# An MLP by seven products per block pair: token halves of 512 and 520 instead of 516 and 516

## The chip, the cores and the metric

One core of a Trainium2 chip. The metric is device time in microseconds (us) of one execution of the whole kernel, as the median of several runs. A profile of one execution stands beside it.

## The reference

A decoder trunk of two layers over 1024 prompt tokens and 8 sample tokens (1032 in all), width 1024, everything in float32. Layer 0 mixes tokens by a gated linear recurrence, layer 1 by sliding-window attention. Each layer ends in an MLP, which is all that the change touches:

```python
def sq_relu_mlp(x, w_up, w_down):
    return jnp.square(jax.nn.relu(x @ w_up)) @ w_down

    ...
        yp = yp + sq_relu_mlp(rms_norm(yp, norm_mlp_g[layer]), mlp_w_up[layer], mlp_w_down[layer])
        ys = ys + sq_relu_mlp(rms_norm(ys, norm_mlp_g[layer]), mlp_w_up[layer], mlp_w_down[layer])
```

`w_up` is 1024 x 4096 and `w_down` 4096 x 1024. The prompt's and the samples' tokens are stacked to 1032 columns, features lie on the 128 partitions.

## The kernel before

**Seven products.** Each MLP is written with Winograd's form of Strassen's scheme: a pair of 128-row blocks of weights and the two halves of the tokens form a 2 x 2 block product, which needs seven products instead of eight. The weights' blocks A11 to A22 are combined into S1 to S4 on VectorE (L498), the tokens' blocks B11 to B22 into T1 to T4. `BY` (L452) says which product uses which operands: 1 is A11 B11, 2 is A12 B21, 3 is S4 B22, 4 is A22 T4, 5 is S1 T1, 6 is S2 T2, 7 is S3 T3. H0 and H1 are the two token halves, both 516 columns wide (`HALF`).

**Three passes.** TensorE takes its operands rounded; to keep float32 accuracy every operand is split into a rounded part and a rest: ScalarE rounds it (a cast, L396 for weights and L402 for stored sums), VectorE subtracts (L397, L403). A product is then three passes, high x high, high x low and low x high, over j blocks of the contraction. Each pass of each j is two matmuls of 258 columns (`QT`), because a bank of PSUM holds 512 float32 columns and 516 don't fit: `product`, L525 to L533.

**Stages.** The up-projection has 16 block pairs q (`NPAIR`), with j over 4 blocks, so 7 x 4 x 3 x 2 = 168 matmuls a pair. The hidden vectors of the first 14 pairs (`NSP`) are combined again, by `sums_of` (L570), and stored to HBM (`hsum`) by DMAs that ScalarE issues; the last two pairs go to `hid` as they are. The down-projection runs over 5 chunks of the contraction (three pairs each, two in the last), with 4 output pairs in each, 126 or 84 matmuls a pair; the output tiles of the first four chunks are added into HBM by accumulating DMAs that GpSimd issues (L656), those of the last chunk take what has been added there (L658). What remains of the contraction, the two pairs in `hid`, follows as a plain matrix product in `down_steps` (L315).

**Order.** `PROG` is the list of products as TensorE runs them, and the loop at L611 goes through it: it makes the operands that are due (`pw.take`), issues the matmuls, evacuates, and asks for the weights' splits of the next products (`pw.look`, by the list `SOON`). The first two pairs are interleaved (their token operands are made at the same time, `tok.make`); after that each pair runs in the order 1, 2, 6, 7, 5, 4, 3. The instructions of an engine are put in an order by the framework's scheduler; `high_priority` and `issue_after` steer it.

**Banks.** PSUM has 8 banks, and a product uses two at a time (`DB`): tag G twice, X once, Y once. Partial sums are shared: U2 = P1 + P6 and so on are accumulated in the bank of an earlier product after ScalarE has copied the earlier value out (L637), and VectorE adds the other ones (L639, L641, L643, L645). The results go to two tiles of a pair, `he` and `ho`, of 1032 columns each. In up, a relu with the norm's factor (L649, VectorE) and a square (L650, ScalarE) follow.

**Loads in the down-projection.** While a chunk runs, `Ahead.fetch` loads the stored sums of the next one (`tl`, L543, DMAs that GpSimd issues), and `Ahead.split` splits them four or five products later. SyncE issues the loads of the weights (L160). Token tiles come from a pool `ap` of 33 buffers, weights' splits from `wp` with 12, and most `he` tiles of the down-projection from the two spare buffers of `rp`.

Of the kernel before, what the change touches and what calls it, by code (L numbers as in the profile page):

```python
# [27 lines left out]
HALF = T // 2  # L28
# [3 lines left out]
QT = T // 4  # L32
# [28 lines left out]
def trunk(ctx: ExitStack, tc: tile.TileContext, I, O):  # L61
# [31 lines left out]

    def A(s="a"):
        return ap.tile([P, T], F32, tag="A", name=nm(s))
# [18 lines left out]
    def DB(tag):  # L114
        return psum["pool"].tile([P, 1024], F32, tag="D" + tag, bufs=2 if tag == "G" else 1, name=nm("bD"))
# [18 lines left out]
    aux = cp.tile([P, CH], F32, name="aux")  # L134
# [255 lines left out]

    H0, H1 = slice(0, HALF), slice(HALF, T)


    def op_of(src, alloc, n):
        t = alloc("op")
        act.copy(r_(t[:, 0:n]), src)  # L396
        dve.tensor_tensor(r_(t[:, n:2 * n]), src, t[:, 0:n], ALU.subtract)  # L397
        return t[:, 0:n], t[:, n:2 * n]
# [8 lines left out]
    class TokenOps:  # L407
        def __init__(self, xs):
            self.pairs = [(xs[2 * j], xs[2 * j + 1]) for j in range(4)]
            self.ops = {n: [] for n in ("B11", "B21", "T3", "T2", "T1", "T4", "B22")}  # L410

# [5 lines left out]
        def early(self, m):  # L417
            j = m // 2
            if m < 4:
                self.make("B11", [m])  # L420
            if m >= 6:
                self.make("B21", (2 * m - 12, 2 * m - 11))
            e, o = self.pairs[j]
            if m % 2 == 0:
                dve.tensor_tensor(e[:, H0], e[:, H1], e[:, H0], ALU.subtract)
            else:
                dve.tensor_tensor(e[:, H1], o[:, H1], e[:, H1], ALU.subtract)

        def B11(self, e, o, j):
            return op_of(e[:, H0], A, HALF)  # L430

        def B21(self, e, o, j):
            return op_of(o[:, H0], A, HALF)

        def B22(self, e, o, j):
            return op_of(o[:, H1], A, HALF)

        def T3(self, e, o, j):
            return op_of(e[:, H1], A, HALF)

        def T2(self, e, o, j):
            dve.tensor_tensor(e[:, H1], o[:, H1], e[:, H0], ALU.subtract)
            return op_of(e[:, H1], A, HALF)

        def T1(self, e, o, j):
            return op_of(e[:, H0], A if j else W, HALF)

        def T4(self, e, o, j):
            dve.tensor_tensor(o[:, H0], o[:, H0], e[:, H1], ALU.subtract)
            return op_of(o[:, H0], A, HALF)  # L450
# [18 lines left out]
    class PairWeights:  # L469
        def __init__(self, layer):  # L470
            self.layer = layer
            self.builds = []
            for key in dict.fromkeys((kind, q) for kind, q, _ in PROG):
                names = ["A11", "A12", "+S1", "+S2", "+S3", "S2", "+S4", "A22", "S3", "S1", "S4"]
                if key in (("up", 0), ("up", 1)):
                    names = ["A11", "A12", "+S1", "+S2", "+S3", "+S4", "A22", "S4", "S3", "S2", "S1"]
                self.builds += [(key, n) for n in names]
            self.src = {}
            self.ops = {}
            self.n = 0  # L480
# [20 lines left out]
        def build(self, upto):  # L501
            while self.n < min(upto, len(self.builds)):
                key, name = self.builds[self.n]
                if name[0] == "+":
                    self.source(key, name[1:])
                else:
                    x = self.source(key, name)
                    self.ops[key, name] = op_of(x, W, self.src[key]["w"])
                self.n += 1
# [15 lines left out]
    def product(d, first, w, xs):  # L525
        n = len(xs)
        for j, (xh, xl) in enumerate(xs):
            for a, (wt, xt) in enumerate(((w[0], xh), (w[0], xl), (w[1], xh))):
                for b in range(2):
                    pe.matmul(d[:, 512 * b:512 * b + QT], lhsT=r_(wt[:, j * P:j * P + P]),  # L530
                              rhs=r_(xt[:, QT * b:QT * b + QT]),
                              start=first and j == 0 and a == 0, stop=j == n - 1 and a == 2,
                              skip_group_check=not first)  # L533
# [7 lines left out]
    def load(src, n):  # L541
        t = A("tl")
        pool.dma_start(t[:, n:2 * n], src)  # L543
        return t[:, 0:n], t[:, n:2 * n]

    PLACE = {n: slice(k * HALF, (k + 1) * HALF) for k, n in enumerate(("B11", "T3", "B21", "B22", "T1", "T2", "T4"))}
# [3 lines left out]
    class Ahead:  # L550
# [6 lines left out]
        def fetch(self, c, upto, step):  # L557
            done = 7 * len(CHUNKS[c]) - len(self.left[c])
            for _ in range(max(0, min(upto - done, len(self.left[c])))):
                name, p = self.left[c].pop(0)  # L560
                self.raw.append((step, c, name, load(self.sums[p][:, PLACE[name]], HALF)))
# [8 lines left out]
    def sums_of(e, o, to):  # L570
        t = small["pool"].tile([P, T], F32, tag="U", name=nm("ts"))

        def put(k, x):
            act.dma_start(to[:, k * HALF:k * HALF + x.shape[1]], x)

        put(2, o)
# [3 lines left out]
        dve.tensor_tensor(t[:, H1], o[:, H1], t[:, H0], ALU.subtract)  # L580
        yield
        put(0, e)
        put(4, t)
        dve.tensor_tensor(o[:, H0], o[:, H0], t[:, H1], ALU.subtract)
        yield
        put(6, o[:, H0])
# [3 lines left out]
    def mlp_products(layer, tok, pw, r, spill, acc, gnext, after):  # L590
# [20 lines left out]
        for n, (kind, q, i) in enumerate(PROG):  # L611
            up = kind == "up"
            w, x = BY[i]
            if up and n in (1, 3, 5, 7, 9):
                tok.make(("B22", "T3", "T2", "T1", "T4")[n // 2])
            if n == 6:
                factors(rs.pop("late"), DB("Y"))
                swap_small(f"u{layer}", 3)
            if (kind, q, i) == ("up", NSP, 5):
# [3 lines left out]
            if i == 1:  # L623
                st[q] = {2: DB("X" if first and q == 1 else "Y"), "g": DB("G"),
                         "e": spare("he") if not up and q in range(2, 12) else A("he"), "o": A("ho")}
            z = st[q]
            alone = i in (1, 2, 7) or (i == 3 and first)
            if alone and i in (3, 7):
                z[i] = DB("Y" if first and q == 0 else "X")
            d = z["g"] if i in (1, 5, 6) else z[7] if i == 4 else z.get(i, z["g"])  # L630
            product(d, alone, wt, (tok if up else ahead).ops[x] if up else ahead.ops[q // 4][x])
            e, o, g = z["e"], z["o"], inner(z["g"])
            e0, e1, o0, o1 = [quarters(t[:, h]) for t in (e, o) for h in (H0, H1)]
            if i in (1, 6, 7, 3):
                t, f = {1: (e0, g), 6: (o0, g), 7: (o1, inner(d)), 3: (e1, inner(d))}[i]
                with tc.high_priority():
                    last["copy"] = act.copy(t, f).ins  # L637
            if i == 2:
                dve.tensor_tensor(e0, inner(d), e0, ALU.add)  # L639
            elif i == 5:  # L640
                dve.tensor_tensor(o1, g, o1, ALU.add)  # L641
                if 3 in z:
                    dve.tensor_tensor(e1, g, e1, ALU.add)  # L643
            elif i == 4:
                dve.tensor_tensor(o0, inner(d), o0, ALU.add)  # L645
            ready = {4: "o", 3: "" if alone else "e", 5: "e" if 3 in z else ""}.get(i, "")
            if ready and up:
                t = z[ready]
                dve.scalar_tensor_tensor(t, t, 0.0, r, ALU.min, ALU.mult)  # L649
                act.activation(t, t, AF.Square)  # L650
                if q >= NSP:
                    act.dma_start(hid[layer][2 * (q - NSP) + (ready == "o")], t)
            elif ready:
                m, t = 2 * (q % 4) + (ready == "o"), z[ready]
# [5 lines left out]
            if i == (4 if 3 in z else 3):  # L660
# [6 lines left out]
            if up and q == NPAIR - 1:  # L667
                k = ORDER.index(i)
                ahead.fetch(0, 3 * (k + 1), n)
                ahead.split(n)  # L670
            elif not up:
                c, k = q // 4, 7 * (q % 4) + ORDER.index(i)
# [591 lines left out]
    hsum = [tc.dram_tile([NSP, P, 7 * HALF], F32, name=f"hsum{i}") for i in range(2)]  # L1264
# [161 lines left out]
```

## Time and profile before

| | us |
|---|---|
| median of 3 runs | 2003.95 (2003.02 to 2004.08) |
| the profiled execution | 2002.95 |
| its span, from the first to the last instruction | 2001.2 |
| TensorE busy | 1987.5 (99%) |
| VectorE busy | 1394.0 (70%) |
| ScalarE busy | 1021.0 (51%) |
| GpSimd busy | 364.4 (18%) |
| TensorE's matmuls of the MLP products (L530), both layers | 648.2 and 568.0 |

The granted clock of TensorE is 1.000 on average. In the profile PE is TensorE's matmuls, PEld its loads of weights, DVE VectorE, ACT ScalarE, POOL GpSimd, SP SyncE; ACTq, SPq and POOLq are DMAs that these engines issue. A group's row reads: line, engine, operation, what is written <- what is read, shape, count | busy us, mean ns of one | idle time of the engine just before them, and what ended it. Matmuls overlap, so that the busy time of a group is less than its count times its mean. The first MLP runs from about 335 to 942 us, the second from about 1344 to 1952 us.

### The profile page before, as it was taken

Reading aid. Unit: us, or ns where it says so; the run is one execution under the profiler, and the core shown is the slowest. Engines: PE = TensorE matmul, PEld = TensorE weight load, DVE = VectorE, ACT = ScalarE, POOL = GpSimd, SP = SyncE. Lnnn points to the kernel's source line nnn. Section 1 sums busy time; section 2 is a strip of 40 time slices with the busy share of each in tenths; the row PEclk is TensorE's granted clock in tenths of the full one; section 3 lists DMA queues with packets and bytes.
Section 4 is the critical chain, followed back from the end, with each engine's and each line's share of the span. In section 5 each row is a group of like instructions: output and inputs, shape, how many; then the busy total and the mean of one; then the engine's idle time right before and its main releaser. Section 6 shows DMA issues by size and latency. Waiting matters only on the chain.

```text
span 2001.2 us, 38937 instructions
## 1 busy us (share of the span) xinstructions
PE 1987.5 (99%) x15188; PEld 1954.1 (98%) x15188; DVE 1394.0 (70%) x2649; ACT 1021.0 (51%) x2021; POOL 364.4 (18%) x664
## 2 busy tenths in 40 slices
PE   9999999999999999999999999999999999999999
PEld 8999999999999999999999897999999999999999
DVE  8996638877675877666846768478767667666662
ACT  7576535543433655545545656455434336554550
POOL 2320000000001233221006658000000003323220
PEclk9999999999999999999999999999999999999999
DMA  5111242343435778877444535623443447888773
GB/s 180 53 43 53 77 147 78 128 164 125 161 127 204 233 211 217 236 198 173 129 106 108 136 98 170 206 81 108 149 154 133 159 149 250 219 221 220 191 194 107
DMA packets 117929, 305.04 MB, mean 152 GB/s; under 512 B 17512, under 2 KB 50032, under 8 KB 117744
## 3 DMA queue, kind: packets, MB, share of 16 engines
q1 hardware_dynamic: 61744, 135.55, 22.0%
q0 software_dynamic: 28352, 98.30, 19.1%
q10 hardware_dynamic: 27648, 68.70, 9.4%
q8 instruction: 119, 1.95, 0.4%
q14 instruction: 66, 0.54, 0.1%
HBM read 176.30 MB, written 113.51 MB: 145 GB/s over the span
## 4 chain that ended last, share of the span: by engine, by line
PE 96%; DVE 1%; POOL 1%; ACT 1%; issue 1%; DMA 0%; SPq 0%; DVEq 0%; POOLq 0%; ACTq 0%
PE bD L530 61%; PE bP L227 13%; PE bS L227 8%; PE bP L793 5%; PE bT L227 4%; PE bS L867 1%; PE bO L916 1%; PE bS L823 1%; PE bT L893 1%; PE bP L893 1%; DMA raw<-w_in 0%; POOL se L883 0%; PE bN L757 0%; DVE sq L278 0%; POOL bias L870 0%
## 5 line engine op out<-in xcount | busy, mean ns | idle before, releaser
L530 PE MATMUL bD<-op,op 128*128 128x258 f32 x5376 | 648.2, 283 | 0.0
L530 PEld LDWEIGHTS bD<-op,op 128*128 128x128 f32 x5376 | 647.7, 190 | 0.3
L530 PE MATMUL bD<-tl,op 128*128 128x258 f32 x4704 | 568.0, 283 | 0.0
L530 PEld LDWEIGHTS bD<-tl,op 128*128 128x128 f32 x4704 | 566.8, 190 | 1.0 <-ACT he L637 0.3
L543 POOL DMA_DIRECT2D tl<-hsum x196 | 115.3, 695 | 899.7 <-PE bD L530 423.0
L397 DVE TENSOR_TENSOR op<-ws,op 128x512 fp32r<-128x512 f32 (+2 forms) x288 | 170.4, 597 | 81.2 <-ACT op L396 81.2
L403 DVE TENSOR_TENSOR tl<-tl 128x516 fp32r<-128x516 f32 x196 | 130.8, 693 | 122.1 <-ACT tl L402 119.5
L637 ACT COPY ho<-bD 128x516 f32<-128x516 f32 x144 | 85.0, 590 | 245.2 <-PE bD L530 240.1
L396 ACT CAST op<-ws 128x512 fp32r<-128x512 f32 (+2 forms) x288 | 155.8, 550 | 56.0 <-DVE op L397 27.1
L397 DVE TENSOR_TENSOR op<-raw,op 128x512 fp32r<-128x512 f32 (+2 forms) x216 | 124.2, 595 | 57.7 <-ACT op L396 57.7
L637 ACT COPY he<-bD 128x516 f32<-128x516 f32 x144 | 83.9, 583 | 133.5 <-PE bD L530 122.2
L396 ACT CAST op<-raw 128x512 fp32r<-128x512 f32 (+2 forms) x216 | 114.5, 549 | 33.4 <-PE bD L530 22.6
L402 ACT CAST tl<-tl 128x516 fp32r<-128x516 f32 x196 | 114.9, 627 | 3.9 <-DMA tl<-hsum 3.8
L650 ACT ACTIVATE ho<-ho 128x1032 f32<-128x1032 f32 x32 | 34.2, 1069 | 107.3 <-DVE ho L649 107.3
L167 DVE TENSOR_TENSOR wl<-raw,wh 128x1024 fp32r<-128x1024 f32 (+1 forms) x57 | 66.0, 1164 | 25.8 <-ACT wh L166 16.6
L876 DVE CUSTOM_DVE_ANT_0 se<-bS,bias,nsink 128x256 f32<-128x256 f32 (+1 forms) x128 | 63.9, 522 | 20.9 <-PE bP L893 7.3
L879 ACT ACTIVATE se<-se,den 128x257 f32<-128x257 f32 (+1 forms) x128 | 62.9, 493 | 29.2 <-DVE den L876 21.7
L166 ACT CAST wh<-raw 128x1024 fp32r<-128x1024 f32 (+1 forms) x60 | 58.6, 987 | 36.9 <-PE bT L227 12.4
L656 POOL DMA_DIRECT2D spill<-ho x32 | 28.4, 889 | 237.7 <-DVE ho L645 229.2
L870 POOL TENSOR_SCALAR bias<-con,aux 128x256 f32<-128x256 f32 (+1 forms) x128 | 64.2, 503 | 41.2 <-DVE den L876 16.8
L793 PE MATMUL bP<-hh,wh 128*128 128x344 f32 x192 | 70.0, 364 | 0.0
L645 DVE TENSOR_TENSOR ho<-bD,ho 128x516 f32<-128x516 f32 x72 | 49.7, 690 | 22.9 <-PE bD L530 22.9
(320 smaller groups left out, 3767.5 us busy)
## 6 DMA issues: line engine op xcount, KB each, us to landing
tl<-hsum POOLq DMA_DIRECT2D x196, 258.0 KB, 8.1
raw<-w_up SPq DMA_DIRECT2D x64, 512.0 KB, 3.7
raw<-w_dn SPq DMA_DIRECT2D x64, 384.0 KB, 6.3
spill<-ho POOLq DMA_DIRECT2D x32, 516.0 KB, 6.6
spill<-he POOLq DMA_DIRECT2D x32, 516.0 KB, 8.6
hsum<-ho ACTq DMA_DIRECT2D x28, 516.0 KB, 3.6
hsum<-he ACTq DMA_DIRECT2D x28, 516.0 KB, 2.7
hsum<-ts ACTq DMA_DIRECT2D x28, 516.0 KB, 3.5
```

Of the source, the lines that this page charges most:

```text
L167: eng.tensor_tensor(r_(lo[:, sl]), raw[:, sl], hi[:, sl], ALU.subtract)
L227: pe.matmul(o, lhsT=r_(wt[:, col(k):col(k) + P]), rhs=r_(xt[:, cs(c)]), start=(k == first and a == 0), stop=(k == final and a == 2))
L396: act.copy(r_(t[:, 0:n]), src)
L397: dve.tensor_tensor(r_(t[:, n:2 * n]), src, t[:, 0:n], ALU.subtract)
L402: act.copy(r_(hi), lo)
L403: dve.tensor_tensor(r_(lo), lo, hi, ALU.subtract)
L530: pe.matmul(d[:, 512 * b:512 * b + QT], lhsT=r_(wt[:, j * P:j * P + P]), rhs=r_(xt[:, QT * b:QT * b + QT]), start=first and j == 0 and a = ...
L543: pool.dma_start(t[:, n:2 * n], src)
L637: last["copy"] = act.copy(t, f).ins
L793: pe.matmul(o, lhsT=r_(wt[:, k * P:k * P + P]), rhs=r_(xt[:, cs(c)]), start=(k == 0 and a == 0), stop=(k == M8 - 1 and a == 2))
L870: pool.tensor_scalar(bias2[:, o - n:o], distM[:, 256 - n:256], fac[:, t % 4, 1, b, u:u + 1], SLOPES[hd[u]], ALU.mult, ALU.mult)
L876: dve.tensor_tensor_reduce(se[:, u, 256 - n:256], s[:, u * 256:u * 256 + n], bias2[:, o - n:o], scale=fac[:, t % 4, 0, b, u:u + 1], scalar ...
```

## The change

The token halves become 512 prompt tokens (H0) and 512 prompt tokens with the 8 samples (H1, 520 columns). Operands of H0 alone (B11, B21, T4) have 512 columns, and their products, 1, 2 and 4, are one matmul of 512 columns for each pass; those with H1 (B22, T1, T2, T3), products 3, 5, 6 and 7, are two of 260. Where blocks of different widths are combined, the samples' columns count as zero in H0: they are copied (8 columns) instead of added, and product 6's evacuation takes product 1's value with 8 columns cleared behind it.

The banks: a single-bank tag Z, twice, for products 1, 2 (added onto 1) and 4; a double-bank tag D, three times, for 6, 7, and 5 with 3 (added onto 5). The steady order becomes 1, 6, 2, 7, 4, 5, 3, with product 1 of the next pair ahead of product 3; the last pair of each projection ends 4, 5, 2, 3. The first two pairs run 1, 2, 3, 7, 6, 4, 5, each product for both. Loads of stored sums follow the new order of use. Tiles of pool `ap` grow from 1032 to 1040 columns; the tile `aux` is given up and lies on the states tile.

The core of the diff:

```diff
-HALF = T // 2
+HW = SEQ // 2
+W1 = T - HW
+TW = 2 * W1
-QT = T // 4
+QT = W1 // 2
...
-    def DB(tag):
-        return psum["pool"].tile([P, 1024], F32, tag="D" + tag, bufs=2 if tag == "G" else 1, name=nm("bD"))
+    def DB():
+        return psum["pool"].tile([P, 1024], F32, tag="D", bufs=3, name=nm("bD"))
+
+    def ZB():
+        return psum["pool"].tile([P, 512], F32, tag="Z", bufs=2, name=nm("bZ"))
...
-    aux = cp.tile([P, CH], F32, name="aux")
...
-    H0, H1 = slice(0, HALF), slice(HALF, T)
+    H0, H1 = slice(0, HW), slice(HW, T)
+    HP, HS = slice(HW, SEQ), slice(SEQ, T)
...
-    ORDER = (1, 2, 6, 7, 5, 4, 3)
+    ORDER = (1, 6, 2, 7, 4, 5, 3)
+    FINAL = (1, 6, 7, 4, 5, 2, 3)
     SOON = (8, 9, 10, 11, 12, 13, 15)
-    PROG = [("up", q, i) for q in (0, 1) for i in (1, 2)] + [("up", q, i) for i in (3, 7, 6, 5, 4) for q in (0, 1)]
-    PROG += [("up", q, i) for q in range(2, NPAIR) for i in ORDER]
+    PROG = [("up", q, i) for i in (1, 2, 3, 7, 6, 4, 5) for q in (0, 1)]
+
+    def steady(kind, qs):
+        out = []
+        for q in qs:
+            for i in ORDER if q != qs[-1] else FINAL:
+                if i == 3 and q != qs[-1]:
+                    out.append((kind, q + 1, 1))
+                if i != 1 or q == qs[0]:
+                    out.append((kind, q, i))
+        return out
+
+    PROG += steady("up", range(2, NPAIR))
     NUP = len(PROG)
-    PROG += [("dn", b, i) for b in range(4 * len(CHUNKS)) for i in ORDER]
+    PROG += steady("dn", range(4 * len(CHUNKS)))
...
-                names = ["A11", "A12", "+S1", "+S2", "+S3", "S2", "+S4", "A22", "S3", "S1", "S4"]
+                names = ["A11", "+S1", "+S2", "S2", "+S3", "+S4", "A12", "S3", "A22", "S1", "S4"]
...
-                for b in range(2):
-                    pe.matmul(d[:, 512 * b:512 * b + QT], lhsT=r_(wt[:, j * P:j * P + P]),
-                              rhs=r_(xt[:, QT * b:QT * b + QT]),
+                c = HW if xt.shape[1] == HW else QT
+                for b in range(xt.shape[1] // c):
+                    pe.matmul(d[:, 512 * b:512 * b + c], lhsT=r_(wt[:, j * P:j * P + P]),
+                              rhs=r_(xt[:, c * b:c * b + c]),
...
-                tok.make(("B22", "T3", "T2", "T1", "T4")[n // 2])
+                tok.make(("B22", "T3", "T2", "T4", "T1")[n // 2])
...
-            d = z["g"] if i in (1, 5, 6) else z[7] if i == 4 else z.get(i, z["g"])
-            product(d, alone, wt, (tok if up else ahead).ops[x] if up else ahead.ops[q // 4][x])
...
-            if i in (1, 6, 7, 3):
-                t, f = {1: (e0, g), 6: (o0, g), 7: (o1, inner(d)), 3: (e1, inner(d))}[i]
-                with tc.high_priority():
-                    last["copy"] = act.copy(t, f).ins
-            if i == 2:
-                dve.tensor_tensor(e0, inner(d), e0, ALU.add)
-            elif i == 5:
-                dve.tensor_tensor(o1, g, o1, ALU.add)
-                if 3 in z:
-                    dve.tensor_tensor(e1, g, e1, ALU.add)
-            elif i == 4:
-                dve.tensor_tensor(o0, inner(d), o0, ALU.add)
...
+            if i == 3 and not first:
+                d = z["d"]
+            elif i in (3, 5, 6, 7):
+                d = z["d"] = DB()
+            else:
+                d = ZB() if i == 4 else z["z"]
+            product(d, i != 2 and (i != 3 or first), wt, tok.ops[x] if up else ahead.ops[q // 4][x])
+            with tc.high_priority():
+                if i == 1:
+                    last["copy"] = act.copy(e0, d).ins
+                elif i == 6 and not first:
+                    with tc.issue_after(last["sum"]):
+                        dve.memset(e[:, HW:W1], 0.0)
+                    dve.tensor_tensor(o1, inner(d), quarters(e[:, 0:W1]), ALU.add)
+                    act.copy(e[:, H1], o[:, H1])
+                elif i == 6:
+                    for t, p in ((o1, o[:, HP]), (e1, e[:, HP])):
+                        dve.tensor_tensor(t, inner(d), t, ALU.add)
+                        dve.tensor_tensor(p, e0, p, ALU.add)
+                    last["copy"] = act.copy(e0, z["z"]).ins
+                elif first and i in (3, 7):
+                    last["copy"] = act.copy(e1 if i == 3 else o1, inner(d)).ins
+                elif i == 4:
+                    dve.tensor_tensor(o0, d, o[:, HP], ALU.add)
+                elif i == 2 and not first:
+                    last["copy"] = act.copy(e0, d).ins
+                else:
+                    for t in ((o1, e1) if first else (e1,) if i == 3 else (o1,)) if i != 2 else ():
+                        last["sum"] = dve.tensor_tensor(t, inner(d), t, ALU.add).ins
...
+    cp8 = cp.tile([P, 4, NS], F32, name="cp8")
     sp.dma_start(st, I["states"])
+    aux = st.rearrange("p m n -> p (m n)")[:, 0:CH]
```

In `sums_of` and in the token operands the samples' columns are handled by copies of 8 columns beside the subtractions, as in

```diff
-        dve.tensor_tensor(t[:, H0], e[:, H1], e[:, H0], ALU.subtract)
+        dve.tensor_tensor(t1, e[:, HP], e[:, H0], ALU.subtract)
+        dve.tensor_copy(t1s, e[:, HS])
```

More of the change, by code (lines that the diff above doesn't have):

```diff
@@ L92, in nm, with A2 @@
         return f"{s}{cnt[0]}"
+    def A2(s="a"):
+        return ap.tile([P, TW], F32, tag="A", name=nm(s))
     def A(s="a"):
-        return ap.tile([P, T], F32, tag="A", name=nm(s))
+        return A2(s)[:, 0:T]
     def W(s="w"):
@@ L388, in out_proj, with op_of @@
         return xs, need, entry_steps(lambda m: ws[m], srcs, xs, gname, r, spill, **kw)
-    H0, H1 = slice(0, HALF), slice(HALF, T)
-    def op_of(src, alloc, n):
+    H0, H1 = slice(0, HW), slice(HW, T)
+    HP, HS = slice(HW, SEQ), slice(SEQ, T)
+    def op_of(src, alloc, *more):
+        n = sum(x.shape[1] for x in (src, *more))
         t = alloc("op")
-        act.copy(r_(t[:, 0:n]), src)
-        dve.tensor_tensor(r_(t[:, n:2 * n]), src, t[:, 0:n], ALU.subtract)
+        at = 0
+        for x in (src, *more):
+            hi, lo = t[:, at:at + x.shape[1]], t[:, n + at:n + at + x.shape[1]]
+            act.copy(r_(hi), x)
+            dve.tensor_tensor(r_(lo), x, hi, ALU.subtract)
+            at += x.shape[1]
         return t[:, 0:n], t[:, n:2 * n]
@@ L410, in __init__ @@
             self.ops = {n: [] for n in ("B11", "B21", "T3", "T2", "T1", "T4", "B22")}
+            self.samples = cp8
         def make(self, name, js=range(4)):
@@ L541, in load @@
     def load(src, n):
-        t = A("tl")
+        t = A2("tl")
         pool.dma_start(t[:, n:2 * n], src)
         return t[:, 0:n], t[:, n:2 * n]
-    PLACE = {n: slice(k * HALF, (k + 1) * HALF) for k, n in enumerate(("B11", "T3", "B21", "B22", "T1", "T2", "T4"))}
+    PLACE = {}
+    for n, w in (("B11", HW), ("T3", W1), ("B21", HW), ("B22", W1), ("T1", W1), ("T2", W1), ("T4", HW)):
+        at = max((x.stop for x in PLACE.values()), default=0)
+        PLACE[n] = slice(at, at + w)
     class Ahead:
@@ L560, in fetch @@
                 name, p = self.left[c].pop(0)
-                self.raw.append((step, c, name, load(self.sums[p][:, PLACE[name]], HALF)))
+                self.raw.append((step, c, name, load(self.sums[p][:, PLACE[name]], PLACE[name].stop - PLACE[name].start)))
         def split(self, step):
@@ L570, in sums_of, with put @@
     def sums_of(e, o, to):
[L571 to L576, printed above, removed]
+        t = small["pool"].tile([P, TW], F32, tag="U", name=nm("ts"))
+        t1, t1s, t2, t2s = [t[:, x] for x in (slice(0, HW), slice(HW, W1), slice(W1, W1 + HW), slice(W1 + HW, TW))]
+        def put(n, x):
+            at = PLACE[n].start
+            act.dma_start(to[:, at:at + x.shape[1]], x)
+        put("B21", o)
         yield
-        dve.tensor_tensor(t[:, H0], e[:, H1], e[:, H0], ALU.subtract)
+        dve.tensor_tensor(t1, e[:, HP], e[:, H0], ALU.subtract)
+        dve.tensor_copy(t1s, e[:, HS])
         dve.tensor_tensor(e[:, H1], o[:, H1], e[:, H1], ALU.subtract)
-        dve.tensor_tensor(t[:, H1], o[:, H1], t[:, H0], ALU.subtract)
+        dve.tensor_tensor(t2, o[:, HP], t1, ALU.subtract)
+        dve.tensor_copy(t2s, e[:, HS])
         yield
-        put(0, e)
-        put(4, t)
-        dve.tensor_tensor(o[:, H0], o[:, H0], t[:, H1], ALU.subtract)
+        put("B11", e)
+        put("T1", t)
+        dve.tensor_tensor(o[:, H0], o[:, H0], t2, ALU.subtract)
         yield
-        put(6, o[:, H0])
+        put("T4", o[:, H0])
     xd = []
@@ L614, in mlp_products @@
             if up and n in (1, 3, 5, 7, 9):
-                tok.make(("B22", "T3", "T2", "T1", "T4")[n // 2])
+                tok.make(("B22", "T3", "T2", "T4", "T1")[n // 2])
             if n == 6:
-                factors(rs.pop("late"), DB("Y"))
+                factors(rs.pop("late"), DB())
                 swap_small(f"u{layer}", 3)
-            if (kind, q, i) == ("up", NSP, 5):
+            if (kind, q, i) == ("up", NSP, 4):
                 swap_small(f"q{layer}", 4)
@@ L623, in mlp_products @@
             if i == 1:
-                st[q] = {2: DB("X" if first and q == 1 else "Y"), "g": DB("G"),
-                         "e": spare("he") if not up and q in range(2, 12) else A("he"), "o": A("ho")}
+                st[q] = {"z": ZB(), "e": spare("he") if not up and q in range(2, 12) else A("he"), "o": A("ho")}
             z = st[q]
-            alone = i in (1, 2, 7) or (i == 3 and first)
-            if alone and i in (3, 7):
-                z[i] = DB("Y" if first and q == 0 else "X")
@@ L638, in mlp_products @@
-            if i == 2:
-                dve.tensor_tensor(e0, inner(d), e0, ALU.add)
-            elif i == 5:
-                dve.tensor_tensor(o1, g, o1, ALU.add)
-                if 3 in z:
-                    dve.tensor_tensor(e1, g, e1, ALU.add)
-            elif i == 4:
-                dve.tensor_tensor(o0, inner(d), o0, ALU.add)
-            ready = {4: "o", 3: "" if alone else "e", 5: "e" if 3 in z else ""}.get(i, "")
-            if ready and up:
-                t = z[ready]
[L649 to L654, printed above, removed]
+            e, o = z["e"], z["o"]
@@ new lines, in mlp_products @@
+            e0, o0 = e[:, H0], o[:, H0]
+            e1, o1 = quarters(e[:, H1]), quarters(o[:, H1])
+            if i == 3 and not first:
[27 more added lines that the diff above has]
+                        last["sum"] = dve.tensor_tensor(t, inner(d), t, ALU.add).ins
@@ new lines, in mlp_products @@
+            done = {5: "oe" if first else "o", 3: "" if first else "e"}.get(i, "")
+            for ready in done:
+                t = z[ready]
+                if up:
+                    dve.scalar_tensor_tensor(t, t, 0.0, r, ALU.min, ALU.mult)
+                    act.activation(t, t, AF.Square)
+                    if q >= NSP:
+                        act.dma_start(hid[layer][2 * (q - NSP) + (ready == "o")], t)
+                    continue
+                m = 2 * (q % 4) + (ready == "o")
@@ L659, in mlp_products @@
                     xs[m] = t
-            if i == (4 if 3 in z else 3):
+            if "e" in done:
                 if up and q < NSP:
@@ L666, in mlp_products @@
                 next(g, None)
-            if up and q == NPAIR - 1:
-                k = ORDER.index(i)
+            if NUP - 7 <= n < NUP:
+                k = n - NUP + 7
                 ahead.fetch(0, 3 * (k + 1), n)
@@ L1263, in trunk @@
     hid = [tc.dram_tile([2 * (NPAIR - NSP), P, T], F32, name=f"hid{i}") for i in range(2)]
-    hsum = [tc.dram_tile([NSP, P, 7 * HALF], F32, name=f"hsum{i}") for i in range(2)]
+    hsum = [tc.dram_tile([NSP, P, 3 * HW + 4 * W1], F32, name=f"hsum{i}") for i in range(2)]
     def ahead(layer):
```

30 lines of the change are left out of this document (14 added, 16 removed).

## The prediction

> **What bounds the kernel now.** I read the page's busy table first, then the chain that ended last, then the groups of instructions by line, then stretches of the span.
>
> ```profile
> span 2001.2 us, 38937 instructions
> PE 1987.5 (99%) x15188; PEld 1954.1 (98%) x15188; DVE 1394.0 (70%) x2649; ACT 1021.0 (51%) x2021; POOL 364.4 (18%) x664
> ...
> L530 PE MATMUL bD<-op,op 128*128 128x258 f32 x5376 | 648.2, 283 | 0.0
> L530 PEld LDWEIGHTS bD<-op,op 128*128 128x128 f32 x5376 | 647.7, 190 | 0.3
> L530 PE MATMUL bD<-tl,op 128*128 128x258 f32 x4704 | 568.0, 283 | 0.0
> L530 PEld LDWEIGHTS bD<-tl,op 128*128 128x128 f32 x4704 | 566.8, 190 | 1.0 <-ACT he L637 0.3
> ```
>
> TensorE is busy 99% of the span. The product groups at L530, the only matmuls that the change touches, hold 648.2 + 568.0 = 1216.2 us in 5376 + 4704 = 10080 matmuls of 258 columns. Their own mean of 283 ns is not what one costs: they overlap. What one costs is its spacing, which the chain of waits in order of time gives (start, length, engine and line, count):
>
> ```profile
> 59.27 11.31 PE bP L227 x72
> ...
> 352.71 590.02 PE bD L530 x4896
> ...
> 1022.26 17.90 PE bS L823 x152
> ...
> 1361.71 590.45 PE bD L530 x4896
> ```
>
> In each MLP 4896 matmuls follow one another without a link of any other engine: 590.02 / 4896 = 120.51 ns for 258 columns. The projection at L227 (344 columns) gives 11.31 / 72 = 157.08 ns, and L823 (256 columns) 17.90 / 152 = 117.76 ns. So 86 columns more cost 36.57 ns, 0.425 ns a column, and the line through 258 and 344 leaves 10.8 ns at no columns: a part of each matmul that does not depend on its width. That is what the change can win. In the two load rows the idle is 0.3 and 1.0 us over both MLPs: nothing else holds the products up. An off-path engine matters only if it becomes late.
>
> **The matmuls.** Before, each pass of each of seven products is two matmuls of 258 columns. Afterwards products 1, 2 and 4 take one of 512, and 3, 5, 6, 7 two of 260. Of 10080 matmuls three sevenths, 4320, become 2160 of 512; 5760 stay, two columns wider.
>
> A 512-column matmul isn't in this trace. Bounds from the rows: two 256s less one fixed part, 2 x 117.76 - 10.8 = 224.7 ns, from below. From above, the slope between the 256 and 344 rows, (157.08 - 117.76) / 88 = 0.447 ns a column, carried on from 344: 157.08 + 168 x 0.447 = 232.1 ns. I take the line through 258 and 344, 157.08 + 168 x 0.425 = 228.5 ns: 344 is the nearest width, and 258 is the same instruction. Two halves now cost 2 x 120.51 = 241.02 ns, so 12.5 ns are saved each time, 2160 x 12.5 = 27.0 us (19.3 to 35.3 by the bounds).
>
> For 260 columns the same line gives 120.51 + 0.85 ns, 5760 x 0.85 = 4.9 us lost. The bounds: 258 costs 2.75 ns more than 256, and if two more columns cost that again, 15.8 us are lost; if instead 258 is an awkward width and 260 lies on the 256-344 line (117.76 + 4 x 0.447 = 119.55), 5.5 us are gained. I keep the line, which needs no such exception.
>
> The matmuls alone: 27.0 - 4.9 = 22.1 us less.
>
> The Trainium skill (TensorE: Matmul & The Clock Gate, "Wait — 56ns, not 53.3ns?") puts the spacing at N/2.4 ns plus about 2.5 ns, all of the fixed part that one wider matmul could save. Its 110.0 ns for 258 columns disagrees with the 120.51 of this trace; by its differences the matmuls would gain only 4.5 us (215.8 ns for 512, 110.8 for 260).
>
> **The evacuations.** Rows by form (mean ns of one):
>
> ```profile
> L645 DVE TENSOR_TENSOR ho<-bD,ho 128x516 f32<-128x516 f32 x72 | 49.7, 690 | 22.9 <-PE bD L530 22.9
> L1236 DVE TENSOR_TENSOR t<-ri,st 128x8 f32<-128x8 f32 x8 | 1.5, 183 | 0.0
> L637 ACT COPY ho<-bD 128x516 f32<-128x516 f32 x144 | 85.0, 590 | 245.2 <-PE bD L530 240.1 <-DMA spill<-ho 5.0
> L637 ACT COPY he<-bD 128x516 f32<-128x516 f32 x144 | 83.9, 583 | 133.5 <-PE bD L530 122.2 <-DVE ws L498 10.6
> ```
>
> A steady pair goes from four VectorE adds and four ScalarE copies to five adds (after 6, 7, 4, 5, 3) and three copies (after 1, 6, 2), one of them SBUF to SBUF. VectorE also gets a clearing of 8 columns, and in the up product two 8-column copies: 0.69 + 3 x 0.18 = 1.2 us a pair in up, 0.9 in down. Where that lies beside the products:
>
> ```profile
> 344.00:387.00 43.00, 43.00 (x357) 42.90 (x356) 41.50 (x65) 24.63 (x43) 0.00 (x0) 1.00 0.24 88
> 450.00:550.00 100.00, 100.00 (x834) 100.00 (x833) 67.80 (x100) 40.16 (x65) 0.00 (x0) 1.00 0.41 143
> 700.00:800.00 100.00, 100.00 (x833) 100.00 (x832) 71.89 (x131) 53.91 (x108) 33.46 (x53) 1.00 0.82 214
> 880.00:942.00 62.00, 62.00 (x515) 61.71 (x514) 43.97 (x85) 35.12 (x70) 12.98 (x18) 1.00 0.75 184
> ```
>
> Columns: stretch, length, then busy us of PE, PEld, DVE, ACT, POOL; clock, DMA share, GB/s. A pair takes 168 x 0.1205 = 20.2 us in up, 126 or 84 matmuls (15.2 or 10.1 us) in down. VectorE goes from 68% to about 75% in up, from 72% to 79% in down, from 71% to 81% in the last four blocks. It stays hidden there. The clock is 1.00 throughout and I leave it there.
>
> **The first two pairs** have no such cover: from 344 to 387 us VectorE is busy 41.50 of 43.00 us. Here the change raises the adds of a pair from four to seven (product 6 now gives four), 2 x 3 x 0.69 = 4.1 us per layer. Also, product 4 needs a single bank, which is freed only when the old sum in it is copied out after those four adds: 4 x 0.69 + 0.58 = 3.3 us behind product 6 of the pair, with only one product of 24 x 121.4 ns = 2.9 us between. That alone is 0.4 us late for each of two pairs. T4's operands (an extra subtraction each) are needed two products sooner, T1's two later. Between 0 and 5 us per layer; I take 2, or 4 us in all, as VectorE's sums of the next weights can be put off.
>
> **Waits and banks in the steady part.** Product 2 lands on product 1's bank, with 3 and 6 between for the copy of 0.58 us. Product 3 adds onto 5's bank: the add of 0.69 us has the next pair's product 1 to itself (12 x 228.5 = 2.7 us in up, 1.4 us in the last four blocks). S2's split is asked for behind product 1's copy and has one product as cover, as before. A11's split for the next pair loses one: it was used two products after it was asked for, now one. The three double banks and the two single ones come round after a whole pair. I cost all this at nothing; the cover is always at least one product, and the 0.3 us of PEld waiting on `he` above shows that one product (2 under 6) suffices now.
>
> **Transfers.** Rows of a stored sum are 3616 columns instead of 3612, 0.1% more bytes. Loads are asked for in the new order of use, at the same steps:
>
> ```profile
> tl<-hsum POOLq DMA_DIRECT2D x196, 258.0 KB, 8.1
> ...
> spill<-he POOLq DMA_DIRECT2D x32, 516.0 KB, 8.6
> ```
>
> A load lands after 8.1 us and its last tile is needed eight products (over 11 us) after it is asked for. The spare `he` buffer comes round after six products, 12.9 us in the long blocks, against 0.69 + 8.6 us of add and accumulation: hidden, but by 3.6 us only. SP's weight loads keep their order and lead. Moving `aux` onto the states tile costs nothing: that tile was stored long before attention.
>
> **Sum.** -27.0 + 4.9 + 4 = -18.1 us. The profiled execution took 2002.95 us (span 2001.2 us), the median of the runs is 1.0 us above it. So 1984.9 us for a profiled execution and 1985.9, say **1986 us**, for the median.
>
> **Rivals.** *Little fixed cost.* The 256 and 344 rows alone give a fixed part of 117.76 - 256 x 0.447 = 3.4 ns. If joining two matmuls saves only that and four columns, 512 costs 241.02 - 3.4 - 1.8 = 235.8 ns, 11.2 us gained; 260 at 0.447 a column loses 5.1 and the first pairs 4: 2 us in all, 2002 us, no change that can be told. For it: the two rows, and the page named above points the same way. Against it: it leaves the step from 256 to 258 unexplained. 0.07.
>
> *A11 comes late.* The next pair's A11 has product 5 alone as cover, and its VectorE subtraction stands behind the add after 4, and perhaps behind splits that wait for ScalarE:
>
> ```profile
> DVE op L397 <- ACT op L396: 141.5, 106, 3.2
> ```
>
> (total us, times, longest.) If one subtraction of 0.69 us sticks out in each of 68 steady pairs, that is 47 us, and 2003.95 - 18 + 47 = 2033 us. It decides from 18.1 / 68 = 0.27 us a pair on. For it: that row, up to 3.2 us once. Against: TensorE's own idle now is about 1 us where S2 has the same cover. 0.10.
>
> **How the numbers follow.** About 0.2% (4 us) is what this measurement can tell from no change. Forecast 0.80, little fixed cost 0.07, A11 late 0.10, some other wait that eats the gain 0.03. The forecast's own range, one unknown at a time: 512 at 224.7 gives 1978, at 232.1 gives 1994; 260 at 119.55 gives 1975.5, at 123.26 gives 1997; the first pairs at 0 or 10 give 1982 and 1992. So 1974 to 1998 holds the forecast and leaves the rivals out. Faster 0.81, same 0.07, slower 0.12.
>
> **What would show it.** Product chains of each MLP near 2 x (1080 x 0.2285 + 2880 x 0.1214) = 1193 us over both instead of 1214.7; rows of 512 columns x2160 and of 260 x5760; the load rows' idle still a few us, most of it in the first 50 us of each MLP, released by VectorE or ScalarE. Right after a steady 512 the spacing tells 228.5 from 235.8. Wrong if TensorE waits for `op` or `he` in every pair, or if spacing at 260 is above 123 ns.

## The result

The changed kernel takes 1982.51 us (median of 4 runs, 1981.91 to 1983.60) against 2003.49 us before in the same comparison (2002.91 to 2004.08): a ratio of 0.9896, 95% interval 0.9879 to 0.9913. 21 us less, where 18 were forecast, inside the stated range. The total was right; its terms were not, as the profile after shows.

The page of the changed kernel (span, busy time by engine, groups of the products; the matmuls' line is now L557):

```profile
span 1980.2 us, 34864 instructions
PE 1966.3 (99%) x13028; PEld 1836.3 (93%) x13028; DVE 1486.5 (75%) x2937; ACT 1001.4 (51%) x1961; POOL 366.2 (18%) x664
...
L557 PE MATMUL bD<-op,op 128*128 128x260 f32 x3072 | 382.7, 282 | 0.0
L557 PE MATMUL bD<-tl,op 128*128 128x260 f32 x2688 | 343.8, 282 | 0.0
L557 PE MATMUL bZ<-op,op 128*128 128x512 f32 x1152 | 282.1, 394 | 0.0
L557 PE MATMUL bZ<-tl,op 128*128 128x512 f32 x1008 | 255.5, 395 | 0.5 <-DVE tl L416 0.5
```

The counts are those of the plan: 1152 + 1008 = 2160 matmuls of 512 columns, 3072 + 2688 = 5760 of 260. TensorE is busy 99% as before, VectorE 75% instead of 70%. The span is 21.0 us shorter. The stretches of the two MLPs, first of the kernel before, then of the changed one (stretch, length, busy PE, PEld, DVE, ACT, POOL):

```profile
335.01:942.73 607.72, 607.72 (x5045) 607.22 (x5044) 433.83 (x717) 300.63 (x549) 88.85 (x141) 1.00 0.59 177
1344.06:1952.16 608.10, 608.10 (x5043) 607.37 (x5043) 435.52 (x721) 301.06 (x550) 88.74 (x141) 1.00 0.60 178
```

```profile
335.19:932.73 597.54, 597.29 (x3964) 547.99 (x3964) 480.33 (x857) 291.12 (x520) 89.75 (x141) 1.00 0.62 182
1333.88:1931.28 597.40, 597.15 (x3965) 548.37 (x3963) 482.15 (x860) 292.09 (x521) 89.59 (x141) 1.00 0.61 182
```

10.2 and 10.7 us, 20.9 us in all: the whole gain lies in the MLPs. VectorE has 46.5 us more to do in each and nothing comes of it. What one matmul costs is again its spacing, from the chain of waits in order of time:

```profile
335.19 11.17 PE bZ L557 x48
...
454.83 5.73 PE bD L557 x48
...
1333.88 11.12 PE bZ L557 x48
...
1493.30 5.76 PE bD L557 x48
```

512 columns take 11.12 / 48 to 11.17 / 48 = 231.7 to 232.7 ns, 232 ns; 260 columns 119.4 to 120.0 ns, 119.7 ns. So 512 came out at the dear end of the bounds, and 260 at the cheap end: it costs less than 258 did (120.51 ns). With these, 2160 x (241.0 - 232) = 19.4 us and 5760 x (120.5 - 119.7) = 4.6 us are gained, 24.0 us; the MLPs show 20.9. Of the remaining 3.1 us, 2.5 are a small stall, found below.

### The profile page after: what moved, and what is told of

Read it like the earlier page. It is cut to its first block, busy times and chain, and to the rows that moved or that the text cites. A ratio compares the mean times of both kernels' runs of the same rounds, so it can differ in the third digit from the quotient of the medians.

```text
span 1980.2 us, 34864 instructions
## 1 busy us (share of the span) xinstructions
PE 1966.3 (99%) x13028; PEld 1836.3 (93%) x13028; DVE 1486.5 (75%) x2937; ACT 1001.4 (51%) x1961; POOL 366.2 (18%) x664
## 4 chain that ended last, share of the span: by engine, by line
PE 93%; DVE 3%; DMA 1%; ACT 1%; issue 1%; POOL 1%; SPq 0%; DVEq 0%; ACTq 0%; POOLq 0%
PE bD L557 34%; PE bZ L557 25%; PE bP L234 12%; PE bS L234 7%; PE bP L840 5%; PE bT L234 3%; PE bS L914 1%; PE bO L963 1%; PE bS L870 1%; PE bT L940 1%; DMA tl<-hsum 1%; PE bP L940 1%; DMA raw<-w_in 0%; POOL se L930 0%; PE bN L804 0%
## 5 line engine op out<-in xcount | busy, mean ns | idle before, releaser
L557 PEld LDWEIGHTS bD<-op,op 128*128 128x128 f32 x3072 | 380.3, 188 | 7.8
L557 PE MATMUL bD<-op,op 128*128 128x260 f32 x3072 | 382.7, 282 | 0.0
L557 PEld LDWEIGHTS bD<-tl,op 128*128 128x128 f32 x2688 | 339.2, 188 | 11.9 <-DVE tl L416 0.4
L557 PE MATMUL bD<-tl,op 128*128 128x260 f32 x2688 | 343.8, 282 | 0.0
L557 PE MATMUL bZ<-op,op 128*128 128x512 f32 x1152 | 282.1, 394 | 0.0
L570 POOL DMA_DIRECT2D tl<-hsum x196 | 117.8, 690 | 875.5 <-PE bD L557 411.9
L557 PE MATMUL bZ<-tl,op 128*128 128x512 f32 x1008 | 255.5, 395 | 0.5 <-DVE tl L416 0.5
L557 PEld LDWEIGHTS bZ<-op,op 128*128 128x128 f32 x1152 | 210.5, 188 | 43.6 <-ACT he L682 0.4
L557 PEld LDWEIGHTS bZ<-tl,op 128*128 128x128 f32 x1008 | 180.7, 188 | 35.2 <-DVE tl L416 1.1
L416 DVE TENSOR_TENSOR tl<-tl 128x520 fp32r<-128x520 f32 (+1 forms) x196 | 127.6, 692 | 78.3 <-ACT tl L415 77.9
L409 DVE TENSOR_TENSOR op<-ws,op 128x512 fp32r<-128x512 f32 (+2 forms) x288 | 166.7, 595 | 3.3 <-ACT op L408 3.1
L409 DVE TENSOR_TENSOR op<-raw,op 128x512 fp32r<-128x512 f32 (+2 forms) x216 | 128.2, 595 | 2.0 <-ACT op L408 1.2
L415 ACT CAST tl<-tl 128x520 fp32r<-128x520 f32 (+1 forms) x196 | 110.2, 626 | 0.0
L923 DVE CUSTOM_DVE_ANT_0 se<-bS,bias,nsink 128x256 f32<-128x256 f32 (+1 forms) x128 | 63.9, 522 | 20.9 <-PE bP L940 7.3
```

The costliest lines, as they stand in the source:

```text
L409: dve.tensor_tensor(r_(lo), x, hi, ALU.subtract)
L415: act.copy(r_(hi), lo)
L416: dve.tensor_tensor(r_(lo), lo, hi, ALU.subtract)
L557: pe.matmul(d[:, 512 * b:512 * b + c], lhsT=r_(wt[:, j * P:j * P + P]), rhs=r_(xt[:, c * b:c * b + c]), start=first and j == 0 and a == 0, ...
L923: dve.tensor_tensor_reduce(se[:, u, 256 - n:256], s[:, u * 256:u * 256 + n], bias2[:, o - n:o], scale=fac[:, t % 4, 0, b, u:u + 1], scalar ...
```

## The experiments

**Where the gain comes from: fewer matmuls, or other widths?** Two readings stood against each other. Theory A is the prediction's: 10.8 ns of every matmul do not depend on its width. Theory B: all widths lie on the line through 256 and 344 columns (3.4 ns + 0.447 ns a column), which gives 232.2 ns for 512 and 119.6 for 260, and 258 alone stands 1.8 ns above it.

*260 + 256 in the kernel before.* No matmul less, no column less, banks and order as before. Only the columns written within the two banks move with the widths (252 to 768, in one piece):

```diff
-                for b in range(2):
-                    pe.matmul(d[:, 512 * b:512 * b + QT], lhsT=r_(wt[:, j * P:j * P + P]),
-                              rhs=r_(xt[:, QT * b:QT * b + QT]),
+                for at, to in ((0, 260), (260, 516)):
+                    pe.matmul(d[:, 252 + at:252 + to], lhsT=r_(wt[:, j * P:j * P + P]),
+                              rhs=r_(xt[:, at:to]),
...
```

> The kernel before, each 516-column half passed as 260 and 256 columns instead of 258 and 258; the same number of matmuls and of columns, banks and order as before. Theory A (the prediction's: a part of 10.8 ns for each matmul that one wide matmul saves, 0.425 ns a column): 121.4 + 119.7 = 241.0 ns for a pair, no change, 2003.5 us. Theory B (one line of 3.4 ns + 0.447 ns a column for all widths but 258, which costs 1.8 ns more than its line): 119.7 + 117.8 = 237.5 ns, 5040 x 3.5 = 18 us less, 1986 us.

Measured: 1989.72 us against 2003.87 (ratio 0.9927, 0.9912 to 0.9942). 14.2 us less without any part of the change but the widths. Its chain in the first MLP:

```profile
352.61 583.41 PE bD L530 x4896
```

583.41 / 4896 = 119.16 ns on average, 1.35 ns less than 258 columns took. Theory A is refuted, B holds at three quarters of its size: if the 260 took 119.7 ns here too, the 256 took 118.6, not 117.8.

*512 as 2 x 256 in the changed kernel.* The reverse: only the number of matmuls.

```diff
-                c = HW if xt.shape[1] == HW else QT
-                for b in range(xt.shape[1] // c):
-                    pe.matmul(d[:, 512 * b:512 * b + c], lhsT=r_(wt[:, j * P:j * P + P]),
+                c, at = (HW // 2, HW // 2) if xt.shape[1] == HW else (QT, 512)
+                for b in range(2):
+                    pe.matmul(d[:, at * b:at * b + c], lhsT=r_(wt[:, j * P:j * P + P]),
...
```

> The changed kernel with products 1, 2 and 4 passed as two matmuls of 256 columns into one bank instead of one of 512; all else as changed. Theory A: two fixed parts instead of one, 2160 x (241.0 - 228.5 ns) = 27 us more, 2009 us. Theory B: 2 x 117.8 = 235.6 against 232 ns, 2160 x 3.6 = 8 us more, 1990 us.

Measured: 1991.39 us, 8.9 us more than the changed kernel. Two products of the chain, first 256, then 260 wide:

```profile
376.06 2.83 PE bZ L557 x24
378.89 2.85 PE bD L557 x24
```

2 x 2.83 / 24 = 235.8 ns against 232: joining two matmuls of the same columns saves 3.8 ns, where the prediction took 10.8 ns for it. (The Trainium skill, TensorE: Matmul & The Clock Gate, "Wait — 56ns, not 53.3ns?", has a fixed part of about 2.5 ns: near these 3.8, and far from the 10.8 of the prediction. Its 215.7 ns for 512 columns is not what this kernel shows, 232.)

**What is wrong with 258?** Its 1032 bytes a partition are not a whole number of 16-byte pieces, and the second half starts 8 bytes off such a piece. First the starts alone:

```diff
-                              rhs=r_(xt[:, QT * b:QT * b + QT]),
+                              rhs=r_(xt[:, 256 * b:256 * b + QT]),
```

> The kernel before, the second matmul of each half reads its 258 columns from column 256 instead of 258, so that all reads start on a multiple of 16 bytes (two columns are passed twice and two left out: the MLP's values change, the work does not). Theory A: no change. Theory B if the width of 258 itself is what costs: 120.5 ns, no change, 2003.5 us. Theory B if the starts 8 bytes off a multiple of 16 are what costs (every second matmul): 118.7 ns on average, 10080 x 1.8 = 18 us less, 1985 us.

Measured: 2006.29 us against 2003.87 (ratio 1.0014, 1.0004 to 1.0023): nothing gained. Its chain:

```profile
352.92 591.30 PE bD L530 x4896
```

120.77 ns: aligned starts don't help a width of 258. Then another width of the same kind:

```diff
-                c = HW if xt.shape[1] == HW else QT
-                for b in range(xt.shape[1] // c):
...
+                whole = xt.shape[1] == HW
+                for at, to in ((0, HW),) if whole else ((0, 262), (262, W1)):
...
```

> The changed kernel with products 3, 5, 6 and 7 passed as 262 and 258 columns instead of 260 and 260. Theory B widened (a width that is no multiple of four columns costs about 1.7 ns more than the line): 3.4 ns for each of 2880 pairs, 10 us more, 1992 us, and a spacing of about 121.3 ns on average for the two against 119.8 for 260. If 258 alone is awkward: 5 us more, 1987 us. Theory C (the widths have nothing to do with it, the gain comes from the new tiles' pitch or the places of the banks): no change, 1982.5 us.

Measured: 1994.94 us, against 1982.48 for the changed kernel in the same group; in single executions TensorE's granted clock was 0.997, and the one at 1.000 took 1991.64. So 9 us more at full clock. Its chain:

```profile
1504.61 5.83 PE bD L557 x48
```

121.5 ns on average instead of 119.7, for the same 520 columns (the clock in this stretch is 1.00). That is theory B widened; theory C, by which the widths have nothing to do with it, is refuted. As a check, 264 + 256, two whole widths, in the same edit:

> The changed kernel with products 3, 5, 6 and 7 passed as 264 and 256 columns. Theory B: both are on the line, so as 260 and 260, 1982.5 us within 2 us; a 256 of 118.0 and a 264 of 121.4 ns would show it. If instead 256 is a favoured width and not 258 an awkward one, about 1 ns less for each of 2880 pairs, 3 us less, 1979.5 us.

Measured: 1984.28 us, 1.8 us above the changed kernel beside it, within the 2 us given. By the starts of the matmuls in its trace the 264 takes 122.1 ns and the 256 118.5, together 240.6 against 240.0 for two of 260 in the changed kernel. The 264 is 0.7 ns above the 121.4 given, which stays unexplained. 256 is not a favoured width, and a pair with 258 and 262 columns costs 2.5 ns more than this one. The columns written lie in one piece here, as in the run with 260 + 256, and nothing is gained by that.

Last, a fitting width from starts that don't fit:

```diff
-                              rhs=r_(xt[:, c * b:c * b + c]),
+                              rhs=r_(xt[:, c * b:c * b + c] if c == HW else xt[:, 2 + 256 * b:2 + 256 * b + c]),
```

> The changed kernel with products 3, 5, 6 and 7 reading their two times 260 columns from columns 2 and 258 instead of 0 and 260, so that their reads start 8 bytes off a multiple of 16 (two columns are left out at each end and two passed twice: the MLP's values change, the work does not). If only the width matters, as 258 columns from aligned starts at 120.8 ns point to: 119.8 ns, no change, 1982.5 us. If starts matter for a width that fits: up to 1.7 ns for each of 5760 matmuls, 10 us more, 1992 us.

Measured: 1995.17 us, 12.7 us more than the changed kernel (four columns, 258 to 261, are passed twice, not two): the expectation taken from the run with aligned starts was wrong. Its groups of 260 columns:

```profile
L557 PE MATMUL bD<-op,op 128*128 128x260 f32 x3072 | 389.8, 284 | 0.0
L557 PE MATMUL bD<-tl,op 128*128 128x260 f32 x2688 | 350.0, 285 | 0.1
```

389.8 + 350.0 - 382.7 - 343.8 = 13.3 us, 2.3 ns for each of 5760. Starts do matter. The runs agree, pair by pair, on one description: a 258-column read cuts one 16-byte piece wherever it starts (at its end from an aligned start, at its start from column 258), so that aligning the starts changed nothing; a 260-column read from 8 bytes off cuts two and costs more still; 256, 260, 264 and 512 from aligned starts cut none. That the hardware reads in such pieces is an inference from these widths and starts, not shown.

Two things stay open. Matmul by matmul the cost lies elsewhere than the description has it: by the starts in the trace of the kernel before, the 258 columns from column 0 take 119.0 ns on average and those from column 258 122.2 ns, so that nearly all of the extra cost lies with the read that starts inside a piece; with aligned starts the two take 120.1 and 121.4 ns. And of the runs that change the time only the one with 260 columns from 8 bytes off changes the reads alone: with 258 and 262 columns what is written to PSUM ends or starts inside 16 bytes too, so that reading and writing aren't separated there.

**Is it the order that makes the shared bank free?** The changed kernel without the next pair's product 1 ahead of 3:

```diff
-                if i == 3 and q != qs[-1]:
-                    out.append((kind, q + 1, 1))
-                if i != 1 or q == qs[0]:
-                    out.append((kind, q, i))
+                out.append((kind, q, i))
```

> The changed kernel without the next pair's product 1 ahead of product 3: each pair runs 1, 6, 2, 7, 4, 5, 3, so that 3 lands on the bank of 5 right behind it. If the cover of one product is what makes that bank's sharing free, TensorE now waits for VectorE's add (0.70 us and about 0.1 to 0.3 us to start and to tell) in each of 68 pairs: 54 to 68 us more, 2037 to 2051 us. If the order is not what hides it (TensorE's queue or the scheduler does): no change, 1982.5 us.

Measured: 2018.01 us (2013.76 to 2024.90; the granted clock was between 0.995 and 0.999). 31 us more than the changed kernel in the best execution, half of what was expected; slower than the kernel before. The waits of its weight loads (total us, times, longest), over the whole execution, then in the first MLP's up-projection (395 to 640 us) and in its down-projection (665 to 960 us):

```profile
PEld bD L554 <- DVE ho L688: 40.0, 45, 4.2
...
PEld bD L554 <- DVE ho L688: 2.7, 9, 0.3
...
PEld bD L554 <- DVE ho L688: 20.4, 13, 4.2
```

That is product 3 waiting for the add of product 5, 45 times. In up a wait is 0.3 us at most, and the chain shows why:

```profile
492.03 0.94 PE bZ L554 x4
492.97 2.98 PE bD L554 x24
495.96 1.85 PE bZ L554 x8
```

The framework's scheduler put 4 of the 12 matmuls of the next product 1 ahead of product 3 by itself, 0.94 us, about what the add of 0.70 us needs. In down the 13 waits take 1.6 us each, more than the add itself, because the add comes late:

```profile
708.78 8.47 DMA tl<-hsum
...
719.61 1.02 DVE op L409 x2
720.63 0.62 DVE ho L688
...
721.29 3.82 PE bD L554 x18
```

Here the chain goes back from the add over splits of weights (L409) to a load. So the expected sum, about one add of 0.70 us in each of 68 pairs, had the price and the number of the waits wrong, and the order written by hand is worth 31 us on top of what the scheduler does by itself.

**Does A11 come late?** The prediction's second rival. The edit is meant to take the last cover away:

```diff
-    SOON = (8, 9, 10, 11, 12, 13, 15)
+    SOON = (8, 9, 10, 11, 11, 13, 15)
```

> The changed kernel with the split of the next pair's A11 asked for behind product 5 instead of behind product 4, so that the cover of one product is gone (product 1 of the next pair is the very next one). The rival of the prediction (A11 comes late) priced what sticks out at 0.69 us a pair: if that cover is what keeps TensorE fed, ScalarE's cast and VectorE's subtraction now stick out by 0.5 to 1.2 us in each of 68 pairs, 34 to 82 us more, 2016 to 2064 us. If the scheduler moves the split ahead on its own, or has slack: no change, 1982.5 us.

Measured: 1982.39 us, no change from 1982.5. In the trace VectorE and ScalarE run through their instructions in the changed kernel's order (on each engine one instruction differs by one place, no split of weights, and as much differs between two executions of the changed kernel), and the splits of weights start at the same distances, to about 0.1 us. So the edit moved no split, the scheduler had set its place, and the cover was never taken away: this run doesn't test the rival. What does is the changed kernel's own profile. These are all the waits of the products' weight loads that it lists, in both MLPs:

```profile
PEld bZ L557 <- DVE tl L416: 1.1, 2, 0.6
...
PEld bZ L557 <- ACT tl L415: 0.4, 2, 0.2
PEld bD L557 <- DVE tl L416: 0.4, 2, 0.2
...
PEld bZ L557 <- ACT he L682: 0.4, 2, 0.2
PEld bD L557 <- ACT tl L415: 0.3, 2, 0.2
...
PEld bD L557 <- DVE ho L691: 0.3, 1, 0.3
```

None waits for a split of weights (`op`), so A11 does not come late. How much cover it needs is not shown.

**The stall that is left.** The changed kernel's chain at the start of the first down-projection:

```profile
653.44 1.97 PE bZ L557 x9
655.41 0.61 DVE tl L416
656.02 1.14 DVE he L696
657.16 0.60 DVE tl L416
...
658.40 0.69 DVE tl L416
659.09 0.04 issue
659.13 1.45 PE bZ L557 x5
```

Here the chain leaves TensorE for VectorE's splits of the loaded sums (`tl`); in the second MLP it goes back over two loads of 7.17 and 6.02 us, the second issued when the first had landed. The four rows with `tl` above are the waits at these two places, 2.2 us in all. Asked for one product earlier:

```diff
-            if NUP - 7 <= n < NUP:
-                k = n - NUP + 7
+            if NUP - 8 <= n < NUP:
+                k = n - NUP + 8
```

> The changed kernel with the loads of the first chunk's stored sums asked for one product earlier. If the 1.3 us that each down-projection loses in its first block come from the request: up to 2.6 us less, 1979.9 us. If the loads wait for free buffers or for GpSimd's queue instead: no change, 1982.5 us.

Measured: 1979.96 us against 1982.48 for the changed kernel on the same chip and 2004.55 for the kernel before (ratio 0.9884, 0.9868 to 0.9901). Its chain over the same place does not leave TensorE:

```profile
653.27 2.09 PE bZ L557 x9
655.36 2.17 PE bD L557 x18
657.53 2.09 PE bZ L557 x9
659.62 2.16 PE bD L557 x18
```

2.5 us less, as expected, and the fastest version of all. The changed kernel itself, run as the measure of its group:

> The changed kernel once more, as the measure for the other kernels of this group on the same chip: 1982.5 us.

Measured: 1982.48 us, ratio 0.9890 (0.9875 to 0.9905).

## Why the prediction was right, and which of its steps were not

**What bounds the kernel: right.** TensorE's chain of products set the time before and after, and 20.9 of 21.0 us lie in it.

**512 columns: mis-sized.** Forecast 228.5 ns and 27.0 us gained; measured 232 ns and 19.4 us. The step that failed is the line through 258 and 344 columns, and with it "That is what the change can win". It was taken because 258 was "the same instruction". 258 was the one row that lies off the line of the others, and so the fixed part came out as 10.8 ns instead of 3.4 to 3.8. The upper bound, 232.1 ns from the rows of 256 and 344, was the right value.

**260 columns: wrong sign.** Forecast +0.85 ns and 4.9 us lost; measured -0.8 ns and 4.6 us gained. The bound named for "258 is an awkward width" (119.55 ns) was the right value. Both failures have one cause, with errors of 7.6 us one way and 9.5 the other; that they nearly cancel is luck. So the total is right by luck in good part: with the small fixed part that the runs show, and without the knowledge that 258 is awkward, the forecast would have been that of the first rival, 2002 us.

**Of the gain,** the parts are: joining two 256s into 512, 2160 x 3.8 = 8.2 us (8.9 in the run that undoes it alone); the widths, the remaining 16 of 24 us (14.2 in the run that changes them alone). Most of the gain is that no width is 258 any more, which the prediction had in one bound only.

**The first two pairs: forecast 4 us lost, none measured.** VectorE is full there, as the first of these stretches of the changed kernel shows (columns as above):

```profile
344.00:387.00 43.00, 43.00 (x303) 40.18 (x302) 42.51 (x76) 22.31 (x41) 0.00 (x0) 1.00 0.21 80
450.00:550.00 100.00, 100.00 (x669) 92.00 (x668) 76.20 (x127) 39.99 (x61) 0.00 (x0) 1.00 0.43 150
700.00:800.00 100.00, 100.00 (x668) 91.96 (x667) 79.73 (x151) 54.40 (x106) 31.51 (x50) 1.00 0.88 227
870.00:932.00 62.00, 62.00 (x418) 56.97 (x417) 52.03 (x102) 33.68 (x67) 14.29 (x20) 1.00 0.85 209
```

But the chain has TensorE without a break:

```profile
352.46 12.69 PE bD L557 x106
365.15 5.82 PE bZ L557 x24
```

106 are the four products 7 and 6 (96) and 10 matmuls of product 5: the scheduler put those ahead of product 4 and so filled the wait for its bank. The loss came instead at a place that the prediction costed at nothing, the first chunk's loads, 2.5 us over both layers by the run that asks for them earlier. There the statement that a load's "last tile is needed eight products" after it is asked for holds for the last product's tiles alone: the code asks for the other tiles of the first chunk seven products ahead, and TensorE waits at the third product. Why the kernel before, which asks as early, has no such wait is not shown. Altogether 27.0 - 4.9 - 4 = 18.1 us were forecast, and 19.4 + 4.6 - 2.5 = 21.5 us come from the parts, against 20.9 in the MLPs.

**The steady waits: right.** The sharing of banks costs TensorE next to nothing (0.4 + 0.3 us in the waits on `he` and `ho` above), and the run without the hoisted product shows that the cover, not slack, is the reason. VectorE's added work stays hidden too: 76%, 80% and 84% in the other three stretches above, where 75, 79 and 81% were forecast. No wait for a `he` buffer shows on TensorE.

**Rivals.** Little fixed cost: its first half is true (joining saves 3.8 ns), its conclusion isn't, because it gave 512 columns the excess of two 258s; the objection written beside it, the unexplained step from 256 to 258, decided. A11 late: no wait for `op` shows, but the run meant to test it left the split where it was.

## What to carry to other kernels

Fit the price of a matmul from several widths before moving between them, and look at the row that lies off the line: here the width in use was the odd one. Choose widths and starts of float32 operands in multiples of four columns; splitting 516 as 260 + 256 instead of 258 + 258 alone brought two thirds of the whole change's gain. When one product is put between a sum's two halves in a shared bank, check that something stands there in every pair: taking it away cost 31 us.

## What the runs showed of the hardware

Not expected: a float32 moving operand that starts or ends inside a 16-byte piece costs 1.4 to 2.3 ns more for each matmul of a pair, on average (258: 1.35 ns above 260 and 256 in its place; 262 and 258: 121.5 ns on average; 260 from 8 bytes off: 122.0; 260 aligned: 119.7). That it is the 16-byte pieces is inferred. And joining two matmuls of 256 columns into one of 512 saves only 3.8 ns of 236, although each brings its own load of weights (15188 loads instead of 13028).
